# Trainium2 decoder trunk: two groups of masked products of the first mixer become one group of twice the width

## The chip, the cores and the metric

One Trainium2 chip, one core of it, one launch. The metric is the time of the whole launch in device microseconds, the median over runs. The engines are called as in the profile: PE (TensorE's products), PEld (its weight loads), DVE (VectorE), ACT (ScalarE), POOL (GpSimd, which here issues the small transfers and clears tiles) and SP (SyncE, which issues the weight stream).

## The reference, cut to what matters

A two-layer decoder trunk over 256 positions of width 2048, in float32. The even layer's mixer joins a time mix of 16 heads ("rwkv") and a gated delta rule of 8 heads ("gdn"); the change touches the first of these alone.

```python
def rwkv7_scan(r, w, k, v, a, b):
    """S_t = S_{t-1} diag(w_t) + (S_{t-1} a_t) b_t^T + v_t k_t^T ;  y_t = S_t r_t."""
    def step(S, inp):
        r_t, w_t, k_t, v_t, a_t, b_t = inp
        sa = jnp.einsum('bhvk,bhk->bhv', S, a_t)
        S = S * w_t[:, :, None, :] + sa[..., None] * b_t[:, :, None, :] + v_t[..., None] * k_t[:, :, None, :]
        return S, jnp.einsum('bhvk,bhk->bhv', S, r_t)
    ...

def even_mixer(x, w_in, w_out, ...):
    hcols = x @ w_in
    ya = rwkv7_mix(a_cols, ...)
    yb = gdn_mix(q, k, v, z, beta_raw, alpha_raw, ...)
    return jnp.concatenate([ya, yb], -1) @ w_out
```

The kernel doesn't step through positions. It works on two chunks of 128 positions: within a chunk the recurrence becomes a triangular system, whose matrices are masked products of the scaled keys with two sets of rows (those of `a`, strictly triangular, and those of `r`, triangular with the diagonal).

## The kernel before, in words

PE does the large products of the whole trunk in one long stream: panels of weights by the transposed activations (`pu`, in `up` and `up2`) and activations by weights (`pd`, in `down`). Every weight is split into a high part `wh` (rounded by ACT) and a low part `wl` (the rest, by DVE), so each float32 product is two or three products in a faster format. I call these `pu` and `pd` products the wide stream. The mixers' small work is put between them.

The order of everything is set while the program is built. `Scheduler` holds estimated costs for each instruction and a clock for each engine; generators such as `rwkv`, `gdn` and the post-processing of panels hand it their instructions in stages (each `yield` ends one). After every wide product `fill` issues the small work that by these estimates can begin by then, that with the lowest start time plus priority first. `need` issues small work until a named result has been issued. On the chip each engine then runs its own list in that order and waits on semaphores, so PE stands still when a small product of its list comes before its operands are there.

The first mixer has four `rwkv` units (`q` 0 to 3, four heads each) and two `gdn` units (`f` 0 and 1). At most four of these side tasks are under way at once. A `rwkv` unit makes `bt` (the scaled keys, held in tile `AA`) and for each chunk `c` a tile `AR[c]`, which holds for both pairs of heads `t` 128 columns of `a` rows followed by 128 columns of `r` rows. Then, in the lines that change:

- `att(AB, bt, 0, strict)` makes 8 products of 128 columns (2 chunks, 2 pairs, 2 heads `e` on the array's two halves of 64 rows) into two PSUM banks `at`, and two masked copies of 512 columns put them into the cleared tiles `AB`.
- `inverse_in` sends `AB` to DRAM, `inverse` reads it back reshaped (`ix`), inverts 16x16 blocks on DVE in 15 steps, sends them through DRAM again (`inv`, then tiles `T`) and joins the blocks with small products `iv`.
- `att(RB, bt, 1, incl)` makes the same 8 products for the `r` rows after the inverse, into `RB`, which is first read by the products `Y`.

After this, for each chunk: a group of products for `KT`, then `R`, three dependent products `s0`, `s1`, `s2` of `solve`, `Y`, a normalisation and a transpose `tT`. The outputs go into tiles `yT` (number 0 to 3 from `rwkv`, 4 and 5 from `gdn` 0, 6 and 7 from `gdn` 1). The mixer's output projection `out0` (`pd` products that read `yT`) runs in three parts (`PARTS0`): all four panels over `yT` 0 to 3, then all over 4 and 5, then all over 6 and 7. Each waits through `need` for the `yT` that it reads. The end of a `gdn` unit's chunk is a chain over several engines: products `O`, then `oc` and `ova` on DVE, `rstd` on POOL, `oc` again on DVE, the transposes `tT<-ident,oc` on PE, `osq` on DVE, `yT` rounded on ACT and its rest on DVE.

All instructions are issued through one helper, so the profile gives line 363 for each; they are told apart by the tiles' names.

Of the kernel before, what the change touches and what calls it, by code (L numbers as in the profile page):

```python
# [465 lines left out]
class Trunk(Scheduler):  # L466
# [744 lines left out]
    def rwkv(self, q, yT):  # L1211

        nc, A = self.nc, self.A
# [6 lines left out]
        tl = lambda p, t: p[:, 256 * t:256 * t + 256]  # L1220
# [9 lines left out]
        for dst, nm, src, bias in ((SG, "w2", 0, "w0"), (AA, "a2", 1, "a0")):  # L1230
            ps = self.psq("lo")
# [11 lines left out]
        ps = self.psq("rT")  # L1243
# [10 lines left out]
        ps = self.psq("lo")  # L1254
# [33 lines left out]
        bt, kt = AA, k  # L1288
# [3 lines left out]
        AR = [self.unit("AR") for _ in range(2)]  # L1292
# [11 lines left out]
        yield  # L1304


        AB = [self.unit("AB") for _ in range(2)]
        m4 = lambda n: n.unsqueeze(1).to_broadcast([128, 4, 128])
        strict, incl = self.msk("att")[:, 0:128], self.msk("att")[:, 128:256]

        def att(out, x, j, mask):

            ps = [self.psq("at") for _ in range(2)]
            for c in range(2):
                for t in range(2):
                    for e in range(2):
                        rows, u = slice(64 * e, 64 * e + 64), 2 * c + t
                        nc.tensor.matmul(ps[e][:, 128 * u:128 * u + 128], tl(x, t)[rows, 128 * c:128 * c + 128], tl(AR[c], t)[rows, 128 * j:128 * j + 128], start=True, stop=True)
            for e in range(2):
                nc.gpsimd.memset(out[e], 0.0)  # L1320
                nc.vector.copy_predicated(v3(out[e], 128), m4(mask), v3(ps[e], 128))
        att(AB, bt, 0, strict)
        sk = yield from self.inverse_in(AB)
        yield
        VT, KB = self.unit("VT"), self.unit("KB")
# [5 lines left out]
        un = lambda x, u: x[:, 128 * u:128 * u + 128]  # L1331
        ab = [un(AB[e], u) for e in range(2) for u in range(4)]
        yield from self.inverse(sk, ab, tt)
        of = lambda l, c: [l[4 * e + 2 * c + t] for t in range(2) for e in range(2)]
        RB = [self.unit("RB") for _ in range(2)]
        att(RB, bt, 1, incl)
        yield
        gn = self.unit("gn")
        nc.gpsimd.dma_start(out=gn[:, 0:256], in_=self.h["gn_g"][256 * q:256 * q + 256].partition_broadcast(128))
        nc.gpsimd.dma_start(out=gn[:, 256:512], in_=self.h["gn_b"][256 * q:256 * q + 256].partition_broadcast(128))  # L1340
# [1 line left out]
        for c in range(2):  # L1342
# [3 lines left out]
            ps = [self.psq("at") for _ in range(2)]  # L1346
            for t in range(2):
                for e in range(2):
                    rows = slice(64 * e, 64 * e + 64)
# [5 lines left out]
            ps = self.psq("R")  # L1355
# [10 lines left out]
            if c == 0:  # L1366
                ps = self.psq("S1")
# [6 lines left out]
                for e in range(2):  # L1374
                    rows = slice(64 * e, 64 * e + 64)
# [6 lines left out]
            for u in range(4):  # L1382
                o = Y[:, 64 * u:64 * u + 64]
                self.halves(o, un(RB[u % 2], 2 * c + u // 2), UU[:, 64 * u:64 * u + 64], start=c == 0, stop=False)
                self.halves(o, un(KT[u % 2], 2 * (u // 2) + 1), vt[:, 64 * u:64 * u + 64], start=False, stop=True)
# [21 lines left out]
            ps = self.tok_T(None, [yc[:, 128 * t:128 * t + 128] for t in range(2)], None)  # L1407
# [95 lines left out]
    def gdn(self, f, yT):  # L1503
# [42 lines left out]

        AB, QT = two("AB"), two("QT")
        for c in range(2):
            for a in range(2):
# [3 lines left out]
                g = lambda x: v3(x[c][:, 256 * a:256 * a + 256], 128)  # L1553
                TT(g(AB), v3(ps, 256)[:, :, 0:128], g(DA), op=ALU.mult)
                TT(g(QT), v3(ps, 256)[:, :, 128:256], g(DQ), op=ALU.mult)
                yield
        sk = yield from self.inverse_in(AB)
        un = lambda x, u: x[:, 128 * u:128 * u + 128]
# [368 lines left out]
def v3(ap, n):  # L1927
    return ap.rearrange("p (a b) -> p a b", b=n)
# [50 lines left out]
```

## Time and profile before

| | |
|---|---|
| time, median of 3 runs | 2929.44 us (2923.05 to 2936.93) |
| the profiled execution's own time | 2921.71 us |
| its span on the core | 2919.9 us |
| PE busy | 2897.0 us (99%) |
| DVE busy | 2158.6 us (74%) |
| ACT busy | 1735.7 us (59%) |
| POOL busy | 192.2 us (7%) |

The span is the profiled time from the first to the last instruction; 1.8 us of the execution's time lie around it. Busy times are sums over the whole span. What a small piece of work is worth is seen only in its own stretch: the first mixer's small work lies between about 100 and 565 us.

### The profile page before, as it was taken

The numbers are of one execution on the slowest core, as the hardware profiler recorded it, in microseconds if no ns is written. First come the engines' busy times: TensorE is split into PE (matmuls) and PEld (weight loads), VectorE is DVE, ScalarE is ACT, GpSimd is POOL, SyncE is SP. The second block draws the span as 40 slices with busy tenths as digits, with TensorE's granted clock in tenths as the row PEclk, the third lists the DMA queues.
The fourth block names the chain that finished last, engine by engine and source line by source line (L and its number), as shares of the span: only waits on it lengthen the run. The fifth ranks groups of instructions, "written<-read, shape, count | busy, mean of one in ns | idle before, by whom it ended". The sixth has DMA issues, their size and how long they took to land.

```text
span 2919.9 us, 48428 instructions
## 1 busy us (share of the span) xinstructions
PE 2897.0 (99%) x16986; PEld 2483.8 (85%) x16986; DVE 2158.6 (74%) x4246; ACT 1735.7 (59%) x3320; POOL 192.2 (7%) x317
## 2 busy tenths in 40 slices
PE   9999999999999999999999999999999999999999
PEld 8888888888888888888898888888888888888887
DVE  6789898797777775557856899855787777765567
ACT  6654564466666665446556778844666666654464
POOL 0133212000000000000000011000000000000000
PEclk9999999999999999999999999999999999999999
DMA  8554456465555556555775554655655555565555
GB/s 274 188 148 135 144 175 205 135 203 188 188 188 188 188 188 223 194 192 184 226 229 193 188 184 159 212 194 193 203 187 188 188 188 186 190 222 191 198 182 195
DMA packets 164949, 556.31 MB, mean 191 GB/s; under 512 B 19416, under 2 KB 32520, under 8 KB 164704
## 3 DMA queue, kind: packets, MB, share of 16 engines
q1 hardware_dynamic: 152128, 514.67, 52.3%
q0 software_dynamic: 12576, 38.55, 4.7%
q8 instruction: 133, 2.18, 0.3%
q14 instruction: 112, 0.92, 0.1%
HBM read 542.80 MB, written 10.34 MB: 189 GB/s over the span
## 4 chain that ended last, share of the span: by engine, by line
PE 93%; issue 2%; DMA 2%; DVE 2%; POOL 1%; ACT 0%; SPq 0%; POOLq 0%; DVEq 0%; ACTq 0%
PE pu L363 53%; PE pd L363 34%; PE s L363 1%; PE iv L363 1%; DMA T<-inv 1%; PE Y L363 1%; PE at L363 1%; PE lg L363 0%; DMA inv<-ix 0%; PE tT L363 0%; PE xt L363 0%; POOL rstd L363 0%; DMA inv<-AB 0%; DVE wl L363 0%; PE R L363 0%
## 5 line engine op out<-in xcount | busy, mean ns | idle before, releaser
L363 DVE TENSOR_TENSOR wl<-wr,wh 128x512 fp32r<-128x512 f32 (+2 forms) x1936 | 1318.6, 683 | 629.2 <-PE pd L363 312.3
L363 ACT CAST wh<-wr 128x512 fp32r<-128x512 f32 (+2 forms) x1936 | 1180.2, 618 | 893.2 <-PE pd L363 450.3
L363 PE MATMUL pu<-h,wh 128*128 128x512 f32 (+1 forms) x2944 | 781.5, 385 | 0.2
L363 PEld LDWEIGHTS pu<-h,wh 128*128 128x128 f32 x2944 | 499.3, 189 | 62.3 <-DVE h L363 0.6
L363 PEld LDWEIGHTS pu<-h,wl 128*128 128x128 f32 x2816 | 437.0, 189 | 57.3
L363 PE MATMUL pu<-h,wl 128*128 128x256 f32 x2816 | 463.8, 281 | 0.0
L363 PE MATMUL pu<-x,wh 128*128 128x512 f32 (+2 forms) x1024 | 281.7, 387 | 6.2 <-ACT wh L363 5.2
L363 PE MATMUL pd<-wh,acth 128*128 128x512 f32 x704 | 273.9, 389 | 0.0
L363 PE MATMUL pd<-wl,acth 128*128 128x512 f32 x704 | 273.9, 389 | 0.0
L363 PE MATMUL pd<-wh,actl 128*128 128x512 f32 x704 | 273.9, 389 | 0.0
L363 PE MATMUL pu<-xT,wh 128*128 128x512 f32 x896 | 249.8, 397 | 1.0 <-ACT xb L363 0.6
L363 PE MATMUL pd<-wh,yT 128*128 128x512 f32 x768 | 241.2, 391 | 0.0
L363 PEld LDWEIGHTS pu<-x,wh 128*128 128x128 f32 (+1 forms) x1024 | 173.0, 189 | 28.5 <-ACT wh L363 5.2
L363 PE MATMUL pu<-x,wl 128*128 128x256 f32 (+1 forms) x960 | 172.7, 288 | 0.0
L363 PEld LDWEIGHTS pu<-xT,wh 128*128 128x128 f32 x896 | 153.2, 188 | 21.6 <-ACT xb L363 0.9
L363 PEld LDWEIGHTS pd<-wh,yT 128*128 128x128 f32 x768 | 144.2, 188 | 30.7 <-issue 1.0
L363 PEld LDWEIGHTS pu<-x,wl 128*128 128x128 f32 (+1 forms) x960 | 150.7, 189 | 20.5 <-issue 1.5
L363 PE MATMUL pd<-wh,h 128*128 128x512 f32 x512 | 162.3, 393 | 0.0
L363 PEld LDWEIGHTS pd<-wh,acth 128*128 128x128 f32 x704 | 132.1, 188 | 27.6
L363 PEld LDWEIGHTS pd<-wl,acth 128*128 128x128 f32 x704 | 132.1, 188 | 27.4
L363 PEld LDWEIGHTS pd<-wh,actl 128*128 128x128 f32 x704 | 132.1, 188 | 27.2
L363 PEld LDWEIGHTS pu<-xT,wl 128*128 128x128 f32 x896 | 137.4, 188 | 19.7 <-issue 0.7
(409 smaller groups left out, 3214.1 us busy)
## 6 DMA issues: line engine op xcount, KB each, us to landing
wr<-in_up SPq DMA_DIRECT2D x336, 512.0 KB, 3.2
wr<-in_dn SPq DMA_DIRECT2D x176, 512.0 KB, 4.3
wr<-in_out SPq DMA_DIRECT2D x96, 512.0 KB, 3.8
wr<-in_inB SPq DMA_DIRECT2D x64, 512.0 KB, 3.5
wr<-in_gw SPq DMA_DIRECT2D x64, 512.0 KB, 4.1
wr<-in_inD SPq DMA_DIRECT2D x64, 512.0 KB, 4.1
wr<-in_inA SPq DMA_DIRECT2D x48, 512.0 KB, 4.2
wr<-in_xbc SPq DMA_DIRECT2D x48, 512.0 KB, 3.6
```

Source lines behind the costliest of these rows:

```text
L363: getattr(x.eng, op.name)(*op.a, **op.k)
```

## The change

The two calls of `att` go. For each chunk there are now 4 products of 256 columns (both sets of rows of `AR[c]` at once), into two banks; from each bank the first 128 columns of each pair are copied under the strict mask into the chunk's half of `AB`, the second 128 under the other mask into the chunk's half of `RB`. Between the chunks stands a `yield`. `RB` is made and cleared before the inverse and not after it.

```diff
-        AB = [self.unit("AB") for _ in range(2)]
-        m4 = lambda n: n.unsqueeze(1).to_broadcast([128, 4, 128])
-        strict, incl = self.msk("att")[:, 0:128], self.msk("att")[:, 128:256]
-
-        def att(out, x, j, mask):
+        AB, RB = [self.unit("AB") for _ in range(2)], [self.unit("RB") for _ in range(2)]
+        for c in range(2):
 
             ps = [self.psq("at") for _ in range(2)]
-            for c in range(2):
-                for t in range(2):
-                    for e in range(2):
-                        rows, u = slice(64 * e, 64 * e + 64), 2 * c + t
-                        nc.tensor.matmul(ps[e][:, 128 * u:128 * u + 128], tl(x, t)[rows, 128 * c:128 * c + 128], tl(AR[c], t)[rows, 128 * j:128 * j + 128], start=True, stop=True)
-            for e in range(2):
-                nc.gpsimd.memset(out[e], 0.0)
-                nc.vector.copy_predicated(v3(out[e], 128), m4(mask), v3(ps[e], 128))
-        att(AB, bt, 0, strict)
+            for t in range(2):
+                for e in range(2):
+                    rows = slice(64 * e, 64 * e + 64)
+                    nc.tensor.matmul(tl(ps[e], t), tl(bt, t)[rows, 128 * c:128 * c + 128], tl(AR[c], t)[rows], start=True, stop=True)
+            for out, j in ((AB, 0), (RB, 1)):
+                mask = self.msk("att")[:, 128 * j:128 * j + 128].unsqueeze(1).to_broadcast([128, 2, 128])
+                for e in range(2):
+                    if c == 0:
+                        nc.gpsimd.memset(out[e], 0.0)
+                    nc.vector.copy_predicated(v3(out[e], 128)[:, 2 * c:2 * c + 2], mask, v3(ps[e], 256)[:, :, 128 * j:128 * j + 128])
+            if c == 0:
+                yield
         sk = yield from self.inverse_in(AB)
...
         yield from self.inverse(sk, ab, tt)
         of = lambda l, c: [l[4 * e + 2 * c + t] for t in range(2) for e in range(2)]
-        RB = [self.unit("RB") for _ in range(2)]
-        att(RB, bt, 1, incl)
-        yield
         gn = self.unit("gn")
```

Because the order is made by estimates, the rest of the first mixer is dealt out anew as well. On PE the two orders differ from unit 0's `at` group on up to the second part of `out0`, and are alike after it. The first place is unit 0's `at` group on PE (the names are those of the code; the `x` tiles are the activations, `x4` counts equal rows):

```order
 L363 MATMUL b_1584<-cc,SQ 128x2 x4
-L363 MATMUL at<-AR,AA 128x128 x8
+L363 MATMUL at<-AR,AA 128x256 x4
 L363 MATMUL pu<-x_96,wl 128x256
 L363 MATMUL pu<-x_97,wl 128x256 x2
 L363 MATMUL pu<-x_98,wh 128x512 x2
 L363 MATMUL pu<-x_99,wh 128x512 x2
+L363 MATMUL at<-AR,AA 128x256 x4
 L363 MATMUL pu<-x_98,wl 128x256 x2
```

The eight narrow products have become four wide ones for chunk 0 at the same place, and four for chunk 1 seven wide-stream products later.

The second place is PE at the start of `out0`'s second part, the first product that reads `yT` 4, made by `gdn` 0. Before (there `yT` 4 is `yT_6315` with its low part `yT_6316`, and `yT_4959` is number 3; the `oc` in the last row but one is `gdn` 1's):

```order
L363 MATMUL pd_6751<-wh_6790,yT_4959 128x512
L363 MATMUL pd_6751<-wl_6812,yT_4959 128x512
L363 MATMUL pd_6751<-wh_6790,yT_4960 128x512
L363 MATMUL pd_6884<-wh_6810,yT_6315 128x512
L363 MATMUL pd_6884<-wl_6831,yT_6315 128x512
L363 MATMUL pd_6884<-wh_6810,yT_6316 128x512
L363 MATMUL pd_6885<-wh_6810,yT_6315 128x512
L363 MATMUL pd_6885<-wl_6831,yT_6315 128x512
L363 MATMUL pd_6885<-wh_6810,yT_6316 128x512
L363 MATMUL tT_6870<-ident_78,oc_6806 128x128 x4
L363 MATMUL pd_6884<-wh_6829,yT_6315 128x512
```

And in the changed kernel (`yT` 4 is `yT_6554` with its low part `yT_6555`, `oc_6749` is `gdn` 0's and `oc_6760` is `gdn` 1's):

```order
L363 MATMUL tT_6824<-ident_78,oc_6760 128x128 x4
L363 MATMUL pd_6689<-wh_6730,yT_5457 128x512
L363 MATMUL pd_6689<-wl_6788,yT_5457 128x512
L363 MATMUL pd_6689<-wh_6730,yT_5458 128x512
L363 MATMUL tT_6870<-ident_78,oc_6749 128x128 x4
L363 MATMUL pd_6860<-wh_6786,yT_6554 128x512
L363 MATMUL pd_6860<-wl_6800,yT_6554 128x512
L363 MATMUL pd_6860<-wh_6786,yT_6555 128x512
L363 MATMUL pd_6861<-wh_6786,yT_6554 128x512
L363 MATMUL pd_6861<-wl_6800,yT_6554 128x512
```

`gdn` 0's last transposes stood 60 wide-stream products ahead of the first product that reads its output (outside these rows); now they stand directly ahead of it, behind those of `gdn` 1.

The third place is DVE in the same stretch of the changed kernel (`pd_6688` and `pd_6689` are sums of a finished panel, `wl` the low parts of weights, `osq_6780` and `yT_6624` belong to `gdn` 1, `ova_6812` and `oc_6749` to `gdn` 0):

```order
L363 TENSOR_REDUCE ova_6812<-osq_6811 128x4 [waits Activation_49]
L363 TENSOR_TENSOR wl_6845<-wr_6655,wh_6830 128x512 [waits PE_49,Activation_49]
L363 SCALAR_TENSOR_TENSOR osq_6780<-tT_6824,pk_79,bz_5597 128x256 [waits DMASW2_49,PE_49]
L363 SCALAR_TENSOR_TENSOR osq_6780<-tT_6824,pk_79,bz_5598 128x256
L363 SCALAR_TENSOR_TENSOR x_6014<-x_6014,pd_6688 128x512
L363 SCALAR_TENSOR_TENSOR x_6018<-x_6018,pd_6689 128x512 [waits PE_49]
L363 TENSOR_TENSOR yT_6624<-osq_6780,yT_6623 128x2x128 [waits Activation_49]
L363 TENSOR_TENSOR yT_6674<-osq_6780,yT_6673 128x2x128 [waits Activation_49]
L363 TENSOR_SCALAR ova_6812<-ova_6812 128x4
L363 TENSOR_TENSOR oc_6749<-oc_6749,rstd_6813 128x512 [waits Pool_49]
L363 TENSOR_TENSOR wl_6883<-wr_6709,wh_6843 128x512 [waits DMAHW2_49]
```

`gdn` 0's chain to its transposes is behind `gdn` 1's on DVE, step by step, where before `gdn` 0 came a whole chunk ahead of it.

## Rows read from the trace of the kernel before

**Rows 1.** The page: its first line, and busy time by engine.
```profile
span 2919.9 us, 48428 instructions
...
PE 2897.0 (99%) x16986; PEld 2483.8 (85%) x16986; DVE 2158.6 (74%) x4246; ACT 1735.7 (59%) x3320; POOL 192.2 (7%) x317
```

**Rows 2.** Busy time of each engine by stretch, with the granted clock.
```profile
core 0: us, PE busy (x) PEld busy (x) DVE busy (x) ACT busy (x) POOL busy (x), PEclk, DMA share, GB/s
...
100.00:200.00 100.00, 99.82 (x746) 86.18 (x746) 85.38 (x210) 59.87 (x124) 29.75 (x44) 1.00 0.55 167
200.00:240.00 40.00, 36.53 (x471) 29.81 (x467) 32.81 (x79) 14.21 (x33) 12.22 (x21) 0.96 0.22 58
240.00:480.00 240.00, 237.91 (x2055) 197.16 (x2056) 214.74 (x519) 136.92 (x276) 59.49 (x96) 1.00 0.53 168
480.00:560.00 80.00, 79.75 (x603) 65.37 (x596) 56.71 (x121) 34.50 (x64) 13.29 (x19) 1.00 0.47 153
```

**Rows 3.** PE's costliest wait from 100 to 560 us: total us, times, longest us.
```profile
PE iv L363 <- DMA T<-inv: 3.5, 4, 2.3
```

**Rows 4.** The tile at: durations in ns (least, median, most).
```profile
L363 PEld LDWEIGHTS at<-AR,AA x128: 182/188/188, 139.9 to 356.0; 64*128 64x128 f32 x128
L363 PE MATMUL at<-AR,AA x128: 269/272/373, 139.9 to 356.1; 64*128 64x128 f32 x128
L363 PE MATMUL at<-AR,Ak x64: 376/376/480, 194.8 to 392.6; 64*128 64x256 f32 x64
```

**Rows 5.** Timeline of PE: groups of at, and what starts behind each.
```profile
139.94 1.16 PE L363 MATMUL at<-AR,AA 64*128 64x128 f32 x16
141.03 0.62 PE L363 MATMUL pu<-x,wl 128*128 128x256 f32 x3
...
194.78 1.13 PE L363 MATMUL at<-AR,Ak 64*128 64x256 f32 x8
195.85 1.13 PE L363 MATMUL lo<-lora,w 96*128 96x256 f32 x4
...
236.77 0.71 PE L363 MATMUL at<-AR,AA 64*128 64x128 f32 x8
237.41 0.67 PE L363 MATMUL s<-RU,AB 64*64 64x64 f32 x8
```

**Rows 6.** Masked copies on DVE, grouped by form: count, busy us, mean ns.
```profile
L363 DVE COPY_PREDICATED AB<-mm,at 128x512 f32<-128x512 uint8 x8 | 5.7, 730 | 0.1
...
L363 DVE COPY_PREDICATED T<-mm,iv 32x256 f32<-32x256 uint8 x12 | 5.2, 433 | 1.0 <-PE iv L363 0.8
```

**Rows 7.** Timeline of DVE: chunk 1 of gdn 0, then of gdn 1.
```profile
526.52 0.69 DVE L363 TENSOR_TENSOR oc<-O,egc 128x512 f32<-128x512 f32 x1 [2.27 <-PE O L363]
...
543.83 0.42 DVE L363 TENSOR_TENSOR yT<-osq,yT 128x256 fp32r<-128x256 f32 x1
...
554.09 0.69 DVE L363 TENSOR_TENSOR oc<-O,egc 128x512 f32<-128x512 f32 x1 [3.86 <-PE O L363]
```

**Rows 8.** Timeline of PE: wide products, and the last transposes of gdn 1.
```profile
559.13 0.62 PE L363 MATMUL pd<-wh,yT 128*128 128x512 f32 x2
...
559.81 0.62 PE L363 MATMUL pd<-wh,yT 128*128 128x512 f32 x2
...
560.81 0.63 PE L363 MATMUL tT<-ident,oc 128*128 128x128 f32 x4
561.19 0.47 PE L363 MATMUL pd<-wh,yT 128*128 128x512 f32 x1
```

**Rows 9.** Timeline of ACT: the last rounding of gdn 1's output.
```profile
563.55 0.74 ACT L363 CAST yT<-osq 128x256 fp32r<-128x256 f32 x2
```

**Rows 10.** Stretches of 2 us behind PE's longest wait, with the clock.
```profile
202.00:204.00 2.00, 0.60 (x5) 0.57 (x6) 0.00 (x0) 1.40 (x5) 0.00 (x0) 1.00 0.60 127
204.00:206.00 2.00, 2.00 (x14) 1.65 (x15) 1.51 (x4) 0.00 (x0) 1.70 (x1) 0.68 0.00 0
206.00:208.00 2.00, 2.00 (x40) 2.00 (x39) 0.00 (x0) 0.37 (x1) 0.06 (x1) 0.50 0.03 8
```

## The prediction, made before the changed kernel was run

> **What bounds the kernel now.** I read the page first: PE is busy for 2897.0 of 2919.9 us, DVE for 2158.6 [rows 1]. So only two things can move the time: how long PE's own list takes, and how long PE stands still. Next came the busy times by stretch, around the first mixer, since the orders differ nowhere else. From 100 to 560 us PE is idle for 0.18 + 3.47 + 2.09 + 0.25 = 6.0 us [rows 2]. Of this 3.5 us are waits for the inverse's tiles T, 2.3 us of them in one piece [rows 3]. Behind that piece the granted clock falls from 2.4 to 1.2 GHz for a short while, after a stretch of 2 us with only 0.60 us of products [rows 10]; the mean of 0.96 over 40 us [rows 2] says that this costs 0.04 x 40 = 1.6 us. So everything that a better order could give back here is 7.6 us, 0.26% of the time. DVE is busy for 85% and 89% of the two long stretches of the mixer [rows 2], yet PE rarely waits for it: the order keeps work in hand.
>
> Last I compared the two orders on PE, counting for each small group how many wide products stand before it.
>
> **The products.** Four units lose 16 products of 128 columns each and gain 8 of 256. The trace has two rows for each product, so 128 rows become 64. A whole group of 16 rows at 128 columns holds PE for 141.03 - 139.94 = 1.09 us, a group of 8 rows at 256 columns for 195.85 - 194.78 = 1.07 us [rows 5]. The columns are the same and the weight loads, 188 ns each [rows 4], are hidden either way. Each unit had two groups and has two: 8 x 0.02 = 0.2 us gained.
>
> The Trainium skill has a rule that promises more: "TensorE: Matmul & The Clock Gate", section "Back-to-back issue gap", gives for a stream of load and product some 81 ns at 128 columns and some 131 ns at 512. An estimate by that page, with a straight line between, is 98 ns at 256 columns, thus 128 x 81 - 64 x 98 ns = 4.1 us gained. The trace disagrees: 1.09 us over 16 rows is 68 ns, 1.07 us over 8 is 133 ns [rows 5], in proportion to the columns.
>
> **Fragments.** A group on part of the array costs something to enter and leave: 8 rows took 237.41 - 236.77 = 0.64 us, 16 rows 1.09 [rows 5], so 0.45 us for 8 more and 0.19 us fixed. Counting in the two orders each change between groups of different array shape, I find 239 before and 227 now: 12 fewer, or 6 visits at 0.19 us, 1.2 us gained at 2.4 GHz.
>
> **The copies.** On DVE 16 copies of 512 columns become 32 of 256. They take 730 ns; a half-size copy under a mask, in the inverse, takes 433 ns [rows 6]. I take that row: 32 x 0.433 - 16 x 0.730 = 2.2 us more DVE work; the other bound, half the price for half the size, is nothing. It is hidden by DVE's idle 14.6 us from 100 to 200 us and 25.3 us from 240 to 480 us [rows 2]; without cover it would cost the 2.2 us. The clears of `RB` are as many as before, on a POOL that is busy for 30 of the 100 us from 100 to 200 us [rows 2], and they come before the inverse's transfers, where POOL waits for DVE anyway. Chunk 1's products come 7 wide products later than before for unit 0, which at 0.68 us for three [rows 8] is at most 1.6 us. The inverse behind them starts later by about that, and what is late next is `R`, with other units' work in between. I price it at nothing; uncovered it would be 1.6 us.
>
> **The new order.** This is the largest term. Unit 2's first `iv` product moves from 1194 wide products to 1456, `gdn` 0's from 1940 to 2056. Nothing waits for these on the way, but `out0` does at its end. Unit 3's last transposes stood 364 wide products ahead of the first reader, now 45, which is still 10 us. `gdn` 0's last transposes stood 60 products ahead, now none: PE reaches the first product of `out0`'s second part right behind them.
>
> So I weigh the chain of `gdn` 0's chunk 1 against what PE has to do meanwhile. From the end of its `O` products PE has 27 wide products, `gdn` 1's transposes, 3 more products, `gdn` 0's transposes, and then three products that read the columns of chunk 0, done long before. With three wide products in 0.68 us and transposes at 561.19 - 560.81 = 0.38 us [rows 8] this is 33 x 0.227 + 2 x 0.38 = 8.2 us. The chain needs at least what `gdn` 1 took alone at the end: 554.09 to 564.29, that is 10.2 us [rows 7, 9]. With two units on DVE it needs more: `gdn` 0's chunk 1 took from 526.52 to 543.83, 17.3 us for 28 DVE instructions of both units and the weights [rows 7], 0.62 us each. In the changed order 21 instructions stand from `oc_6749`'s first to its low part, 21 x 0.62 = 13.0 us. So PE waits 2.0 us at least, 9.1 us at most, and I take 13.0 - 8.2 = 4.8 us, the count of this very stretch. In the kernel before, PE has next to no idle time in this stretch (0.25 us from 480 to 560 us) [rows 2].
>
> A pause of 2.3 us was followed by a fall of the clock [rows 3, 10], so I expect one here too: 1.6 us; the other bound is none.
>
> **The sum** against the profiled execution's 2921.71 us (span 2919.9 and 1.8 around it): -0.2 - 1.2 + 0 (copies) + 4.8 + 1.6 = +5.0 us, 2926.7 us. That execution lay 7.7 us below the median of the three runs, so for the median I add 5.0 to 2929.44: about 2934 us.
>
> **Rivals.**
> - *The order gains.* The wait at `out0` is at its lower bound, the clock stays up, and the pauses of the inverse vanish from the new order: in favour, the waits of before come from four of the inverses' tiles [rows 3] and those move apart. At the very best -1.4 - 6.0 - 1.6 = -9.0 us, 2920; more likely -1.4 + 2.0 - 2.3 - 1.6 = -3.3 us, 2926. Against it: the new order has six inverses too, with the same transfers.
> - *Weight loads bound the narrow products.* If each of the 64 loads that go had been paid in full, 64 x 0.188 = 12.0 us would go [rows 4], 2917. Against it: 16 loads of 188 ns are 3.0 us and the group takes 1.09 [rows 5]. By the rule of the Trainium skill's page "TensorE: Matmul & The Clock Gate" above it would be 4.1 us, 2925.
> - *Slower beyond noise.* Both `gdn` units now go through inverse, chunk 0 and chunk 1 side by side. From `gdn` 0's first `iv` product to `out0`'s second part there were 236 wide products, now 120. Being two costs a chunk 17.3 - 10.2 = 7.1 us [rows 7, 9]. If chunk 0 runs as late against the order as chunk 1 at its upper bound, PE waits 9.1 + 7.1 = 16.2 us, with two falls of the clock 3.2 more: -1.4 + 19.4 = +18.0 us, 2947. It decides from 14.4 us of waiting on (with one fall of the clock). Against it: the other unit's products stand in PE's list as cover, with groups of about a microsecond each.
> - *It changes nothing*: the wait at `out0` is eaten by an earlier pause that goes, 2928 to 2931.
>
> **How the numbers follow.** The likeliest, a wait at `out0` of 2 to 9 us with or without the clock, gives 2929.44 - 1.4 + 2.0 = 2930 to 2929.44 - 1.4 + 9.1 + 1.6 = 2939: 0.50. Order gains or no change, 2920 to 2931: 0.34. Weight loads: 0.02. Slower by more than 0.5%: 0.14. A measurement of this kernel tells about 0.5% (14.6 us) from no change, and the three runs shown spread by nearly that much; all the idle time of the stretch and the clock together are less, so faster is 0.03, slower 0.14, the same 0.83. The range goes from 2922, within the gains, to 2945, where the slow case begins.
>
> **What would show it.** In the changed profile: `at<-AR,AA` only with 256 columns, 64 rows, about 1.07 us a group; 32 copies near 430 ns; PE's list of waits with an entry for `yT` or for `tT` behind `oc` of 3 to 6 us near 560 us, and the clock halved behind it; the rest of the span as before. I am wrong if PE has no idle time there, if the group takes clearly less than 1.07 us, or if the time from 100 to 570 us moves by more than 10 us.

## The result, and the profile after

The changed kernel takes 2946.1 us (median of 6 runs, 2934.7 to 2949.2), the kernel before 2926.7 us in 6 runs beside them: a ratio of 1.0057, with an interval of 1.0044 to 1.0071. It is slower by 17 to 19 us, just over the half per cent that can be told from no change. The forecast was 2934 us, 2922 to 2945.

The page of the kernel after, to be set beside [rows 1]:

```profile
span 2945.0 us, 48329 instructions
...
PE 2910.3 (99%) x16922; PEld 2489.7 (85%) x16922; DVE 2157.3 (73%) x4262; ACT 1732.3 (59%) x3318; POOL 194.3 (7%) x317
```

TensorE has 64 rows less and is busy for 13 us more. The stretches of the first mixer, for [rows 2], show both halves of the loss:

```profile
core 0: us, PE busy (x) PEld busy (x) DVE busy (x) ACT busy (x) POOL busy (x), PEclk, DMA share, GB/s
100.00:200.00 100.00, 97.53 (x699) 83.09 (x698) 80.90 (x210) 55.85 (x115) 27.90 (x42) 0.98 0.54 161
200.00:240.00 40.00, 36.74 (x440) 29.25 (x438) 26.89 (x60) 14.65 (x33) 11.85 (x18) 0.85 0.25 72
240.00:480.00 240.00, 234.93 (x1850) 192.55 (x1851) 208.49 (x518) 130.53 (x266) 53.49 (x84) 0.96 0.51 157
480.00:560.00 80.00, 77.94 (x693) 63.83 (x692) 58.94 (x135) 34.08 (x65) 21.02 (x31) 0.98 0.51 163
560.00:580.00 20.00, 17.68 (x111) 14.19 (x109) 13.48 (x26) 7.91 (x14) 1.26 (x2) 1.00 0.32 103
```

The clock, 0.96 in one of these stretches and 1.00 in the others before, is now under 1.00 in all but the last. PE's waits from 100 to 640 us (total, times, longest), for [rows 3], where T stood at 3.5 us:

```profile
PE iv L363 <- DMA T<-inv: 7.5, 5, 3.8
PE tT L363 <- DVE oc L363: 4.6, 1, 4.6
PE R L363 <- DVE KT L363: 4.1, 5, 1.2
PE tT L363 <- DVE ys L363: 1.0, 2, 0.6
```

The second row is the wait at `out0` that was forecast, and the clock falls behind it. On PE's timeline:

```profile
577.28 0.40 PE L363 MATMUL pd<-wh,yT 128*128 128x512 f32 x1
582.31 0.75 PE L363 MATMUL tT<-ident,oc 128*128 128x128 f32 x4 [4.64 <-DVE oc L363]
582.72 0.77 PE L363 MATMUL pd<-wh,yT 128*128 128x512 f32 x1
```

What was not forecast is that the clock falls five times, for 41 us in all against 3.4 us before. Windows over the five stretches:

```profile
183.40:186.80 3.40, 3.40 (x36) 2.92 (x30) 1.13 (x4) 1.16 (x2) 0.00 (x0) 0.50 0.07 14
227.80:251.70 23.90, 23.38 (x166) 18.06 (x165) 12.58 (x36) 4.93 (x13) 3.00 (x6) 0.50 0.08 24
347.20:354.10 6.90, 5.90 (x42) 4.74 (x42) 2.50 (x7) 0.63 (x2) 0.00 (x0) 0.51 0.38 93
524.70:528.10 3.40, 3.40 (x23) 2.30 (x22) 1.53 (x3) 1.78 (x3) 0.00 (x0) 0.50 0.00 0
582.70:586.20 3.50, 3.50 (x11) 2.52 (x10) 2.91 (x6) 1.66 (x4) 0.00 (x0) 0.51 0.00 0
```

PE is busy in them for 39.6 us, work of 19.8 us at 2.4 GHz. The second fall costs most. It begins behind three pauses for the masked keys:

```profile
224.05 0.67 PE L363 MATMUL R<-SD,AR 128*128 128x128 f32 x4
225.94 0.34 PE L363 MATMUL R<-VT,KT 128*64 128x64 f32 x4 [1.22 <-DVE KT L363]
227.15 0.69 PE L363 MATMUL R<-VT,KT 128*64 128x64 f32 x16 [0.87 <-DVE KT L363]
228.36 0.91 PE L363 MATMUL R<-VT,KT 128*64 128x64 f32 x12 [0.52 <-DVE KT L363]
```

Behind them PE runs only small products up to 250 us, busy all the time, and the clock stays at 1.2 GHz until the wide ones are back:

```profile
203.00:215.00 12.00, 11.82 (x214) 10.22 (x214) 6.14 (x16) 5.48 (x13) 2.48 (x5) 1.00 0.19 66
...
224.00:229.00 5.00, 2.39 (x38) 1.92 (x37) 4.97 (x10) 0.37 (x1) 1.27 (x2) 0.88 0.28 65
229.00:241.00 12.00, 12.00 (x96) 9.59 (x93) 4.79 (x15) 1.47 (x4) 0.00 (x0) 0.50 0.11 41
241.00:250.00 9.00, 9.00 (x58) 6.52 (x59) 5.26 (x15) 3.12 (x8) 3.00 (x6) 0.50 0.01 2
250.00:254.00 4.00, 4.00 (x24) 3.39 (x23) 2.85 (x8) 0.90 (x2) 0.00 (x0) 0.79 0.00 0
```

The wide products are back at 250.25 us, the clock at 251.7. From 203 to 215 us PE also had only small products, with the last long pause (0.75 us) 4 us before them, and the clock stayed up.

Wide products aren't what ends every fall. Behind the first one the clock was back at 186.8 us, and PE ran small products until 188.28:

```profile
186.80:188.20 1.40, 1.40 (x41) 1.34 (x39) 0.06 (x1) 1.24 (x3) 0.00 (x0) 1.00 0.06 12
```

**Two sums that the rest uses.** First, each timed run comes with its mean granted clock. Taking (1 - clock) x span off its time leaves about what it would have taken at 2.4 GHz throughout, or less, since time in which PE stood still at the low clock is taken off as well: here "clock-free". The profiled run is 2946.73 - 0.008 x 2945 = 2923.2 us, the shortest run of the same program 2934.7 - 0.004 x 2933 = 2923.0 us. So the 12 us between them are the clock. The six runs give 2922.6 to 2924.9, median 2923.4; the kernel before gives 2919.4 to 2920.8 as medians on three chips. Clock-free the change costs some 3 to 4 us by these medians; the rest is the clock's. (The clock is given to 0.001, 3 us, so single runs scatter.)

Second, for the profiled executions, from 20 us to the first product of the block behind `out0`: PE's pauses, half of its busy time at 1.2 GHz ("lost"), its other busy time ("work"), and the changes between groups of different array shape that the trace shows (these from the start of the span). Each row is one execution.

```
run            to the block  pauses  lost  work   shape changes
before            603.5        6.0    1.7  575.8      269
after             628.0       17.5   19.7  570.8      256
e1_wide           621.0       16.3   10.1  574.6      258
e2_move           637.2       23.6   21.9  571.6      248
e3_prio           635.5       24.9   14.1  576.5      272
e4_cap            637.7       13.0    6.8  597.9      360
e5_hold           623.3       13.2   16.8  573.3      261
e6_warm           613.9        4.1    0.0  589.8      258
e7_cap4           614.6        8.7   10.2  575.7      271
e8_lat210         608.1        8.4    1.7  578.0      285
e9_holdfed        610.7        4.8    3.2  582.7      261
e10_latefed       611.4        5.7    3.2  582.4      261
e11_beforefed     603.3        3.4    0.0  579.9      269
e12_movehold      607.2        7.6    5.0  574.6      265
```

After against before: 11.5 us of pauses, 18.0 us lost to the clock, 5.0 us less work, together 24.5 of the 25.1 us between the spans. Without the clock's part that is 6.5 us in this pair of executions, more than the 3 to 4 of the medians.

### The profile page after: what moved, and what is told of

It is laid out like the page before. It is cut to its first block, busy times and chain, and to the rows that moved or that the text cites. A ratio compares the mean times of both kernels' runs of the same rounds, so it can differ in the third digit from the quotient of the medians.

```text
span 2945.0 us, 48329 instructions
## 1 busy us (share of the span) xinstructions
PE 2910.3 (99%) x16922; PEld 2489.7 (85%) x16922; DVE 2157.3 (73%) x4262; ACT 1732.3 (59%) x3318; POOL 194.3 (7%) x317
## 4 chain that ended last, share of the span: by engine, by line
PE 94%; issue 2%; DVE 2%; DMA 1%; POOL 1%; ACT 0%; SPq 0%; POOLq 0%; DVEq 0%; ACTq 0%
PE pu L363 54%; PE pd L363 34%; PE s L363 1%; PE Y L363 1%; PE at L363 1%; PE iv L363 1%; PE tT L363 1%; PE lo L363 1%; DMA T<-inv 1%; PE lg L363 0%; PE xt L363 0%; POOL rstd L363 0%; DMA inv<-ix 0%; DVE wl L363 0%; PE R L363 0%
```

## The experiments

The theories: **A**, the new order makes pauses, and these pull the clock down; **B**, the merged products and the half-size copies cost by themselves; **C**, any new order costs as much. Ratios are against the kernel before, run beside each.

**e1_wide: products ahead of two of the pauses.** Ahead of two `R` groups:

```diff
+ if x is self.tensor and op.a[0].tensor.name.split("_")[0] == "R" and op.a[0].tensor.name not in self.fed:
+     self.fed.append(op.a[0].tensor.name)
+     if len(self.fed) in (2, 3):
+         for i in range(6):
+             x.eng.matmul(self.bank_of[op.a[0].tensor.name], self.x0[i][:, 0:128], self.x0[i], start=True, stop=True, skip_group_check=True)
```

> The changed kernel with the same order of its instructions on every engine, and 12 more wide products (128 columns of rows by 512, read by nobody, overwritten by the group behind them) on TensorE: 6 ahead of each of the 2nd and 3rd of the groups R that stood behind a pause at 227 and 228 us. They are 12 x 0.227 = 2.7 us of work. Theory A (the loss is TensorE's pauses and the falls of its clock, above all the 23.9 us at 1.2 GHz that begin at 227.8 us): the pauses are filled or the clock recovers early, 12 us come back, less 2.7 us of added work: about 9 us under the slower executions of the changed kernel (2947), 2936 to 2938. Theory B (the merged products and halved copies themselves cost): unchanged to +2.7 us, 2946 to 2950.

Measured: 2934.0 us (2930.7 to 2939.9), ratio 1.0028 (1.0018 to 1.0039): 12 us under the changed kernel, with 2.7 us more to do, and 2 us under the range that A gave. The long fall is gone:

```profile
220.00:232.00 12.00, 10.75 (x76) 8.02 (x77) 11.87 (x20) 3.33 (x9) 6.12 (x10) 1.00 0.36 97
232.00:244.00 12.00, 12.00 (x162) 9.55 (x162) 8.15 (x25) 4.50 (x12) 1.63 (x4) 1.00 0.10 38
```

PE gets through 162 rows in 12 us of small products, where it was 96 in the 12 us from 229 above. Of the three pauses for the masked keys, 2.6 us, one of 0.8 us is left; with 0.5 us for another tile it makes the 1.25 us idle in the first row. So the edit took pauses away and put wide products in their places: it shows what the fall cost, not which of the two kept the clock up.

**e2_move: the move without the merging**, in the kernel before, scheduled anew.

```diff
  att(AB, bt, 0, strict)
+ RB = [self.unit("RB") for _ in range(2)]
+ att(RB, bt, 1, incl)
  sk = yield from self.inverse_in(AB)
...
- RB = [self.unit("RB") for _ in range(2)]
- att(RB, bt, 1, incl)
- yield
```

> The kernel before, with its two groups of products at 128 columns both ahead of the inverse, unmerged, copies at full size: the move alone. Theory A (the order): the products that keep the clock up are used up as early as in the changed kernel, with small products alone for about 10 us of estimated time near the same place; falls of the clock and a wait of some 4 us at the second part of out0 as in the changed kernel: 2938 to 2950. Theory B (merged products, halved copies): as the kernel before, 2925 to 2930. Theory C (any change of the order moves the time by about 10 us either way, with no place of its own): anything from 2920 to 2950, and falls at other places.

Measured: 2954.7 us (2947.3 to 2957.7), ratio 1.0097: worse than the change itself, without one merged product, and above all three ranges. B alone can't explain the loss. The waits are at the places forecast for an order of this kind, and a fall of 20.5 us begins at 229.4 us:

```profile
PE tT L363 <- DVE oc L363: 7.0, 2, 5.3
PE iv L363 <- DMA T<-inv: 4.4, 3, 2.3
PE R L363 <- DVE KT L363: 4.2, 6, 1.2
```

**e3_prio: `gdn` 0 earlier.**

```diff
- PRIO0 = {("gdn", 1): 0.0}
+ PRIO0 = {("gdn", 0): -100.0, ("gdn", 1): 0.0}
```

> The changed kernel with the last unit but one of the first mixer given a higher rank, so that its last transposes stand some 90 and more wide products ahead of the second part of out0. The first half of the mixer is as in the changed kernel. Theory A: the wait of 4.6 us at out0 and the fall of the clock behind it (3.4 us at 1.2 GHz, 1.7 us lost) go, the long fall at 228 us stays: 6 us under the changed kernel, 2940 to 2941 in its slower executions. Theory B: no change, within 2 us. Rival to the price of the wait: the order is changed so that another tile is late in its place, and nothing is gained.

Measured: 2955.7 us (2950.5 to 2958.2), ratio 1.0101. The wait on `oc` fell from 4.6 to 0.7 us, and another tile was late in its place, unit 3's last transposes, for 14.5 us:

```profile
PE tT L363 <- DVE ys L363: 14.5, 1, 14.5
...
PE tT L363 <- DVE oc L363: 0.7, 1, 0.7
```

The rival to the price held, and 10 us were lost on the changed kernel: the edit made another tile the last, and doesn't show what the wait alone is worth.

**e4_cap: at most 1 us of small products between two wide ones.**

```diff
  def fill(self):
-     while True:
+     t0 = self.tensor.t
+     while self.tensor.t - t0 < 1000:
```

> The changed kernel, with at most 1 us (estimated) of the mixer's small products between two wide ones, so that no stretch of small products alone lasts longer than 1.5 us. Theory A: the long fall at 228 us goes, some 12 us, and maybe the pauses at R with it; the wait at out0 may stay or grow, since the small work is spread later: 2930 to 2937. Theory B: the merged products are all there, and so is the loss: 2943 to 2950.

Measured: 2967.1 us (2959.3 to 2968.2), ratio 1.0137, the slowest of all, though the long fall went as A said:

```profile
200.00:240.00 40.00, 36.69 (x396) 27.47 (x395) 27.01 (x55) 15.85 (x35) 15.31 (x24) 1.00 0.38 93
240.00:480.00 240.00, 240.00 (x1856) 192.63 (x1856) 210.12 (x519) 136.22 (x274) 51.73 (x81) 1.00 0.51 159
```

From 240 to 480 us PE has no pause and the full clock, and the time is lost in the work itself: by the table 27.1 us more, with 104 more changes of array shape. If the changes are all of it, that is 0.26 us each, an estimate. The expectation left this price out, and the time lies above the ranges of both theories.

**e5_hold: the merged work in the order of the kernel before.** The sequence of the kernel before was written down, and is replayed: the merged group stands where `AB`'s stood, the places of `RB`'s group are skipped.

```diff
+ def replay(self):
+     for n in self.script.pop(0):
...
+         goal = merged(task.seen) if task.gen.__name__ == "rwkv" else task.seen + 1
+         task.seen += 1
+         while task.gone < goal:
+             op = self.head(task)
+             self.issue((0, self.start(op) or op.x.t, task, op))
```

> The changed computation in the order of the kernel before: the products of 256 columns stand where the strict-mask products stood (both chunks next to one another), the four masked copies of each chunk on VectorE where the two copies of AB stood, and every other instruction of every engine is in the sequence of the kernel before. Theory A (the loss lies in the new order, not in the merged work): as the kernel before within 3 us, 2922 to 2929, at best 2 us under it, since 8 changes of array shape go. Theory B (merged products and half-size copies cost): slower than before by up to the 17 to 20 us of the changed kernel, 2935 to 2946.

Measured: 2934.3 us, 12 runs from 2922.8 (clock 0.999) to 2941.8 (clock 0.994); ratio 1.0028 (1.0018 to 1.0038). Between the two: half the loss is there in the old order. Clock-free its runs have a median of 2919.6 us, and the kernel before in the same session 2919.9: by the medians what it loses is the clock's. The profiled execution, the slowest of the twelve, has 7.2 us more pauses than the kernel before too, and 2.5 us less work. Its costliest pauses:

```profile
PE iv L363 <- DMA T<-inv: 5.7, 4, 3.2
PE s L363 <- DVE sw L363: 3.3, 2, 2.9
```

The copies of the first chunk into `RB` now stand ahead of the second chunk's copies into `AB`, which the inverse waits for. POOL's timeline has the first unit's start in the kernel before, in e5 and in the changed kernel:

```profile
142.81 1.53 POOL L363 DMA_DIRECT2D inv<-AB  x2 [24.97 <-DVE AB L363]
...
144.02 1.53 POOL L363 DMA_DIRECT2D inv<-AB  x2 [25.17 <-DVE AB L363]
...
145.18 1.53 POOL L363 DMA_DIRECT2D inv<-AB  x2 [26.44 <-DVE AB L363]
```

It is 1.2 us late in e5, and 2.4 us in the changed kernel.

**e6_warm: every large pause of the changed kernel filled**, in its own order. `fed` names the groups that wait, and half the number of products to put ahead.

```diff
+ self.fed = {"iv_2222": 5, "iv_2223": 3, "R_2799": 13, "R_2818": 4, "iv_4194": 17, "iv_6373": 8, "tT_6970": 20}
...
+     for _ in range(2 * self.fed.pop(n, 0)):
+         x.eng.matmul(self.bank_of[n][:, 0:256], self.last.a[1], self.last.a[2][:, 0:256], start=True, stop=True, skip_group_check=True)
```

> The changed kernel in its own order, with 140 products of 256 columns that nobody reads (each repeats the last wide product's operands into the bank of the group that is about to wait, and is overwritten) ahead of seven groups that waited: the iv groups at 181, 183, 348 and 523 us, two R groups at 226 us, and the transposes of gdn 0 at 582 us. They are 16 us of work, put where TensorE stood still for 13 to 14 us. If the pauses pull the clock down (theory A): the five falls go, 18 us come back, and the added work costs 2 to 3 us beyond the pauses it fills: 2929 to 2933, against 2946 for the changed kernel. If the clock falls for another reason: 2946 to 2950, and the falls are still there.

Measured: 2932.0 us, 11 runs from 2931.4 to 2934.4; ratio 1.0023 (1.0015 to 1.0032). With 16 us of needless work the changed kernel is 14 us faster, as A said; none of the five falls is left, and its runs agree within 3 us where they spread over 14. Windows from 100 us to the end of the mixer:

```profile
100.00:613.86 513.86, 509.78 (x4121) 424.71 (x4120) 424.38 (x1002) 263.73 (x526) 116.93 (x177) 1.00 0.51 154
```

**e7_cap4: e4's limit at 4 us.**

```diff
+     while self.tensor.t - t0 < 4000:
```

> As e4_cap, with a limit of 4 us (estimated) in place of 1 us: 16 changes of array shape more than the changed kernel, in place of 124, the longest stretch of small products 3.5 us. Theory A with fragments at e4_cap's price (27 us of busy time for 124 changes, 0.22 us each): 3.5 us of fragments, the long fall gone (12 us), the last transposes 15 wide products ahead of their reader so that the wait at out0 is under 3 us: 2930 to 2938. Rival: another tile becomes late, 2945 and more, as in e3_prio.

Measured: 2933.0 us (2928.0 to 2936.7), ratio 1.0022 (1.0013 to 1.0031), as A said. The wait on `oc` and the long fall are gone, the pauses are 8.7 us, and the work is 4.9 us over the changed kernel's. Three shorter falls, 20.5 us in all, still cost 10.2 us. This is the change with useful work only, and it still doesn't beat the kernel before.

**e8_lat210: another order of the kernel before.**

```diff
- LAT = 190.0
+ LAT = 210.0
```

> The kernel before with no change to what it computes; only the latency that its scheduler assumes between engines is 210 in place of 190 ns, which reorders the small work of the first mixer (15 changes of array shape more). If any new order costs what the change's cost (theory C): 10 to 30 us slower than before, 2936 to 2955, by pauses and falls of the clock at new places. If only the change's own order is bad: within 6 us of before, 2925 to 2932, the more so as no stretch of small products alone is over 3.4 us and the transposes of gdn are not next to their readers.

Measured: 2930.9 us (2924.2 to 2933.8), ratio 1.0013 (1.0005 to 1.0022). A new order cost 5 us, not 20: against C. But it is one order: of the six that were dealt anew, e8 and e7 cost 5 and 7 us, and the change itself, e2, e3 and e4 19 to 42. Whether the order of before is a lucky one among many stays open.

**e9_holdfed and e10_latefed: e5's pauses filled; then the inverse's transfers ahead of the second chunk's copies into `RB`.** e9 adds e6's products ahead of four groups; e10 moves one line further:

```diff
  for out, j in ((AB, 0), (RB, 1)):
+     if j and c:
+         sk = yield from self.inverse_in(AB)
...
- sk = yield from self.inverse_in(AB)
```

> e5_hold with products that nobody reads put ahead of the four groups that waited in it (as 512 columns: 12 ahead of iv at 180 us, 5 ahead of R at 230, 5 ahead of iv at 480, 8 ahead of s2 at 500 us; 6.8 us of work where TensorE stood still for 8.7). If e5_hold's 8 us over the kernel before, and the 19 us between its runs, come from falls of the clock behind these pauses: clock 0.999 or more in all runs, the spread under 5 us, 2924 to 2928. If the merged work costs by itself: 2934 and more, with the clock up.

> e9_holdfed with one move: the copies of the second chunk into RB and nothing else stand behind the two transfers that start the inverse, in place of ahead of them, so that the inverse starts some 0.8 us earlier in each of the four units. If the start of the inverse, 1.2 us later in e5_hold than in the kernel before, is what makes T late: the wait at the first iv group shrinks and 1 us comes back, 2923 to 2927. If the wait is the other work's (transfers, order): same as e9_holdfed within 1 us.

Measured: e9 2931.2 us (2925.3 to 2937.4), ratio 1.0020 (1.0012 to 1.0029); e10 2929.7 us (2927.1 to 2931.5), ratio 1.0014 (1.0005 to 1.0023). The clock rose (0.995 to 0.999 in e9) but not to 0.999 in all runs, and the filling costs by itself: the first expectation of e9 is missed by 3 us. e10 has the sign that was expected, but the intervals overlap, and its first transfers start only 0.4 us earlier (144.17 against 144.56 us). Not told apart.

**e11_beforefed: the kernel before with its pauses filled**, by e6's products ahead of three groups.

> The kernel before with products that nobody reads ahead of three groups that waited in it (as 512 columns: 10 ahead of iv at 201 us, 4 ahead of R at 226, 3 ahead of iv at 468 us; 3.9 us of work where TensorE stood still for 4.1). It is the control for e9_holdfed, and by theory A faster than the kernel before although it does more work: the clock stays up, 2920 to 2923 against 2925.7, with a spread under 4 us. If pauses of this size cost nothing but themselves: 2925 to 2928.

Measured: 2927.5 us (2921.9 to 2929.3), ratio 1.0001 (0.9992 to 1.0010). The clock is up (0.998 to 1.000), the time is the same: what it gave was spent on the added products. A's forecast of a gain is wrong here; a short fall is worth no more than its cure.

**e12_movehold: the move without the merging, in the order of the kernel before.** It is e2's edit, with e5's replay.

> The kernel before in its own order, with one move: the second group of products at 128 columns, its two clears and its two full-size copies into RB stand right behind those of AB, ahead of the inverse; nothing is merged. Set beside e5_hold (the same place, merged, copies of half size; 8 us slower than before) it tells the place from the merging. If the earlier work ahead of the inverse costs (two copies, 1.4 us later start of the inverse in each unit): 2931 to 2937, with waits for T and sw and falls of the clock as in e5_hold. If merged products or half-size copies cost: as the kernel before, 2924 to 2928.

Measured: 2928.5 us (2925.5 to 2934.7), 4.5 us over the kernel before in the same session (2924.0), ratio 1.0011 (1.0001 to 1.0022); clock-free 2918.2 against 2920.8. It falls between its two expectations, with about half of e5's loss. But the inverse is held up less than the expectation had it: the transfers of the first unit start 0.1 us late (142.93 us), those of the second 1.4, against 1.2 and 2.3 in e5. Whether the rest of e5's loss is the merging's, the later start's or the chance of the falls stays open.

**Pauses and falls, over all the traces.** Each of the changed kernel's five falls has a pause of 0.5 us or more within it or up to 2 us ahead, and e6, with wide products in the places of the large pauses, has no fall. But a fall also came without any pause. In e4 PE stood still nowhere from 132 us on; from 139 us it ran small groups with single wide products between them, and at 142.6 us the clock fell:

```profile
132.00:142.60 10.60, 10.60 (x62) 8.68 (x62) 9.40 (x25) 5.81 (x13) 0.00 (x0) 1.00 0.60 197
142.60:149.40 6.80, 6.80 (x22) 4.74 (x19) 4.75 (x11) 1.11 (x2) 1.53 (x2) 0.50 0.26 78
```

And a pause came without a fall, in e12:

```profile
471.48 0.32 PE L363 MATMUL iv<-T,AB 64*64 64x64 f32 x2 [2.33 <-DMA T<-inv]
...
472.00:480.00 8.00, 7.96 (x111) 6.08 (x112) 5.05 (x12) 1.78 (x3) 1.68 (x3) 1.00 0.26 77
```

Nor does the program alone set how long a fall lasts: up to 226 us e1 has the changed kernel's own instructions, and its first fall lasted 10.2 us, not 3.4. So the runs show what pauses and falls cost, and that wide products in the places of the pauses keep the clock up. They don't show that the pause, and not the lack of wide products, starts a fall; the same products at places without a pause were not tried.

## Why the prediction was right or wrong

The direction was right, the size was not: +5.0 us forecast, 17 to 19 measured, and the median lies 1.1 us above the range. The place was right for 6.3 us (4.6 of waiting and 1.7 of the clock) of the 29.5 us by which pauses and clock grew in the profiled execution. How near the time came is in part chance: two of the six runs, 2934.7 and 2935.3 us at a clock of 0.996, stand where the forecast stood, the other four, at 0.991 to 0.993, 11 to 15 us above. Term by term, against the profiled execution:

- **Products, -0.2.** Right. A group of 8 rows at 256 columns takes 266.03 - 264.96 = 1.07 us again, as in [rows 5]:

```profile
264.96 1.13 PE L363 MATMUL at<-AR,AA 64*128 64x256 f32 x8
266.03 0.62 PE L363 MATMUL pu<-x,wl 128*128 128x256 f32 x3
```

  e5 and e12, with and without the merging, have 573.3 and 574.6 us of work with 4 changes of shape between them, 1.0 us at 0.26, so about 0.3 us for the products. The weight loads were hidden either way. The 4.1 us, the estimate from the figures of the Trainium skill's page "TensorE: Matmul & The Clock Gate", section "Back-to-back issue gap", are not there.
- **Fragments, -1.2.** Too small. I priced a visit at 0.19 us; e4 gives 0.26 us a change, 0.5 a visit. With the 13 changes fewer that the trace shows, that is 3.4 of the 5.0 us of work saved; the rest is unexplained. The price is rough: by the table e8 has 16 changes more than the kernel before and 2.2 us more work, 0.14 each, e7 15 more than the changed kernel and 4.9 us, 0.33 each.
- **Copies, 0.** The size was right, and no wait in PE's list names them. 32 copies take 2.1 us more than the 16 of [rows 6]:

```profile
L363 DVE COPY_PREDICATED AB<-mm,at 128x256 f32<-128x256 uint8 x16 | 6.9, 440 | 0.5 <-PE at L363 0.5
L363 DVE COPY_PREDICATED RB<-mm,at 128x256 f32<-128x256 uint8 x16 | 6.9, 438 | 0.0
```

  But I bounded the later start of the inverse by 1.6 us, and let it vanish in other work. It was 2.4 us for the first unit, and PE waited 7.5 us for T where the kernel before has 3.5; how much of that is the later start's isn't shown.
- **The wait at `out0`, +4.8.** Right: 4.6 us, at the transposes of `gdn` 0, behind the chain that was weighed.
- **A fall behind it, +1.6.** Right for this fall: 3.5 us at 1.2 GHz, 1.7 us lost.

**The step that failed** is the sentence "Nothing waits for these on the way, but `out0` does at its end", and with it the sum's one fall of the clock. On the way PE waited 6.9 us more (11.5 - 4.6), above all for T and for the masked keys. The waits for the keys are 4.1 us in the changed kernel, and in the kernel before:

```profile
PE R L363 <- DVE KT L363: 1.0, 1, 1.0
```

And the clock took another 16.3 us (18.0 - 1.7), 12 of them in one fall (half of 23.4). I had read a price for a fall from [rows 10], 1.6 us, and used it as the price of any. There the clock was back at 208.1 us, after 2.7 us with small products alone, and the next wide product came behind that:

```profile
208.35 0.36 PE L363 MATMUL pu<-x,wl 128*128 128x256 f32 x1
```

In the changed kernel it stayed low for seven times as long. e1, where this fall doesn't come, is 12 us faster, and e6, where none comes, 14; why one fall is long and another short isn't shown.

**The rivals.** "Slower beyond noise" came closest (2947 us), by a mechanism that was half right: its 16.2 us of waits were 11.5, of which `gdn` made 4.6 at `out0` and 1.8 for its T (at 522.7 us), and its two falls at 3.2 us were five at 19.8. "The order gains" counted on the pauses of the inverse to go; they doubled. Leaving out the clock, the sum was -1.4 + 4.8 = +3.4 us, and clock-free the kernels differ by 3 to 4 (6.5 in the profiled executions). That it came so near is partly luck: of the pauses that I missed, 6.9 us, the work saved that I missed, 3.6 us, took back half.

## What to carry to other kernels

A pause of TensorE can cost far more than itself, and one fall of the clock doesn't price the next: a fall took 1.7 us here and 12 us there, and the same instructions had 3.4 us at the low clock in one execution and 10.2 in another. The three falls that took most of PE's busy time (the changed kernel, e2, e3: 20.5 to 23.9 us) all lay in one long stretch of small products behind pauses. So after a change that moves small work, look in the new order for such stretches and for what can be late at their start, take a range for the clock and not one number, and read time and granted clock together before blaming the changed lines. A limit on such stretches helped while it was loose: at 1 us (e4) the work grew by 27 us, at 4 us (e7) the long fall went for 5.

## What the runs showed of the hardware

- The clock stayed at 1.2 GHz for 23.9 us with PE busy for 23.4 of them, almost all on small products; it rose 1.4 us after the wide ones were back. e2 and e3 show falls of 20.5 and 23.9 us in the same stretch. It is no rule: from 203 to 215 us small products of the same kind ran at 2.4 GHz, and the first fall of the changed kernel and that of the kernel before ended with small products running.
- Pauses of 1.2, 0.9 and 0.5 us within 4 us came ahead of that fall: no long wait was needed. In e4 the clock fell for 6.8 us with no pause at all ahead, and in e12 it stayed up behind a pause of 2.3 us.
- The same program on one core ran at mean clocks of 0.991 to 0.996, 2949 to 2935 us. With its pauses filled the clock was 0.999 or 1.000 in all 11 runs.
- In e3's pause of 14.5 us the clock fell for 17.1 us, but most of these passed while PE still stood still, so that the fall itself cost little:

```profile
523.00:540.00 17.00, 3.88 (x10) 2.40 (x10) 10.55 (x31) 1.34 (x3) 5.75 (x8) 0.52 0.17 39
```
